# Moving a quarter of the retention's value projection into the turn after the first FFN, with the retention's first loads and key splits placed anew

## The chip, the cores and the metric

The kernel runs on one core of a Trainium2 chip. The metric is the device time of one execution in microseconds (us), as a median of runs. The engines are called as in the profile: PE is TensorE (PEld its weight loads), DVE is VectorE, ACT is ScalarE, POOL is GpSimd, SP is SyncE, which issues most DMAs.

## What is computed

One layer of an encoder on 1024 tokens of width 1024, float32 in and out. Cut to what matters here:

```python
h = swiglu(rms_norm(x), ffn1);  x = x + 0.5 * rms_norm(h)
u = rms_norm(x)
rq, rk, rv, rg, nq, nk, nv, g_ret, g_na = split(u @ w_mix_in)
y = bidirectional_retention(rotary(rq), rotary(rk), rv)   # 4 heads, keys 128, values 256
y_ret = (silu(rg) * headnorm(y)) @ w_ret_out
y_na  = neighbourhood_attention(nq, nk, nv) @ w_na_out     # 8 heads of 64
x = x + rms_norm((sigmoid(g_ret) * y_ret + sigmoid(g_na) * y_na) @ w_mix_out)
h = swiglu(rms_norm(x), ffn2);  x = x + 0.5 * rms_norm(h)
```

The retention runs over 8 chunks of 128 tokens a head, backward for the state that comes from later tokens and then forward.

## The kernel before

All float32 products are made of two parts a value: `split` (lines 61 to 63) writes a rounded high part with a cast on ACT (L62) and the rest as the low part with a subtraction on DVE (L63). `mm3` (L89 to L91) is one product: three matmuls, high by high, high by low and low by high. A weight piece of 128x512 comes by `raw` (L73, a DMA of 512 KB on the SP queue into a ring of four `wraw` buffers), and `load_w` splits it into two pieces, each in one of eight `wh` and eight `wl` buffers.

The work stands in stages: FFN 1 in and out (Winograd products of 2x2 blocks), **the turn**, the mixing projections `mx.run`, neighbourhood attention (`na_cores`), retention (`ret_cores`), output projections, FFN 2.

**The turn** is the stretch in which `ffn_out` has made its last product and the next projection needs the normalised and transposed x. `Epilogue.steps` (L661 to L681) normalises the rows of token tiles 4 to 7, adds the residual `xs[t]`, stores x1 (L670, an SP DMA) and normalises again (L680); `flip` (L128) transposes on PE; `Winograd.put` (L265 to L296) turns each transposed tile into the Winograd operands a22, s1 to s4, with eleven DVE and six ACT instructions a tile. The residuals `xs[t]` of tiles 4 to 7 are loaded by `xload` (L702) into `wraw` buffers, those of tiles 0 to 3 into the weight tiles of `ffn_out` that are no longer needed. Beside the flips runs a filler (`Filler`, a generator whose every step is one `mm3`): `first()` (L1330) makes the values nv of the attention for tokens 0 to 511 (32 steps, `vproj`) and the first products of `mx` (`leads`, 24 steps). FLIP_FILL says how many steps stand ahead of each of the four flips (8) and between a flip and its last split (2); the rest, 16 of the 56 steps, is drained behind them.

**Attention and retention** are fed with another filler, `products()` (L1410): the retention's values rv (`vproj(wrv[j], ...)`, two column halves j, token groups of 3, 3 and 2 tiles, 128 steps), then the gates (16 steps a row block, one `load_w` each), then the output projection of the attention. In all it has 384 steps. `na_cores` runs 32 units, takes 12 steps ahead and 2 + 2 a unit (NA_FILL), 148 in all. `ret_cores` takes what RET_FILL says: 14 at its start; in each head 2 ahead of the backward updates, 2 behind each of the seven updates, 4 and 2 ahead of the forward chunks, 3 and 1 in each of the eight chunks; that is 14 + 4 x 54 + 4 = 234. `fill.drain()` makes the last two.

A retention head needs: `kraw` and `qraw` (loaded by `load`, L1063, one buffer each), the transposed and decayed keys (`kdec.half(g)`: four transposes on PE, L1095, and splits with a scale on ACT and DVE, L65 and L66), the splits of keys and queries (`split_qk`), value chunks by `vget` (L1081 and a split). `half(1)` covers chunks 4 to 7, `half(0)` chunks 0 to 3. In the kernel before, `half(1)` of the next head stands in the last forward chunk, and `half(0)` at the head's start. In a forward chunk PE makes the scores of the next chunk, the filler's steps, the state update, and the cross and inner products; `norm` (L1125 to L1140) works on ACT, DVE and POOL.

The order within each engine's queue is not the text's order alone: Tile's scheduler issues whatever instruction of an engine is ready first by its own estimates, the earlier in the text having priority. SP's queue is one queue: a DMA that waits for its buffer holds up those behind it. Pools are stacked in SBUF; a tile of a new pool waits for the old tiles at its addresses.

Of the kernel before, what the change touches and what calls it, by code (L numbers as in the profile page):

```python
# [28 lines left out]
NHP = 4  # L29

NA_FILL = (12, 2, 2)
RET_FILL = (14, 2, 2, 4, 2, 3, 0, 1, 2)
FLIP_FILL = (8, 8, 8, 8, 2)
LOADS = (6, 9, 12, 15, 18, 22, 28, 33, 38)
NA_UNITS = ((0, 0, 0), (3, 1, 0), (1, 0, 1), (1, 0, 2), (4, 1, 1), (4, 1, 2), (2, 0, 3), (5, 1, 3))
KEY_OFF = (0, 8, 24, 32)
# [3 lines left out]
class Core:  # L40
# [4 lines left out]


    def __init__(self, tc, const, wpool, psum, dram):
        self.tc, self.nc = tc, tc.nc
        self.const, self.wpool, self.psum, self.dram = const, wpool, psum, dram
        nc = self.nc  # L50
        self.ident = const.tile([P, P], F32, name="ident")
        make_identity(nc, self.ident)
        self.mhalf = const.tile([P, 8], F32, name="mhalf")
        nc.gpsimd.memset(self.mhalf, -0.5)
        self.small = None
# [14 lines left out]

    def raw(self, src, n=D):
        raw = self.wpool.tile([P, D], F32, tag="wraw", name="wraw", bufs=4)
        self.nc.sync.dma_start(raw[:, :n], src)  # L73
        return raw

    def piece(self, src, eng=None):

# [332 lines left out]
class Pairs:  # L410
# [273 lines left out]
def ffn_out(c, tiles, q, blocks, w_out, gl, ep, tail, side={}):  # L684
# [16 lines left out]

    def xload(t):  # L702

        if t < 4 or ep.pre is None:
            tile = (tiles[0][1] + tiles[0][0])[t // 2]
            xs[t] = tile[:, t % 2 * 2:t % 2 * 2 + 2].rearrange("p k f -> p (k f)")
            nc.sync.dma_start(xs[t], ep.resid(t))
        else:
            xs[t] = c.raw(ep.resid(t))


    order = []
# [340 lines left out]
def ret_cores(c, pool, spool, d, dec, fill, n):  # L1053
# [2 lines left out]
    nc = c.nc  # L1056
    NC = TT

    def load(h):
        raw = {}  # L1060
        for q in "kq":
            raw[q] = pool.tile([P, S], F32, tag=f"{q}raw", name=f"{q}raw", bufs=1)
            nc.sync.dma_start(raw[q], d[f"r{q}"][h])  # L1063
        return raw

    def split_qk(raw):
# [7 lines left out]
    def vchunks(h):  # L1074
        vraw = {}

        def get(cc):
            if cc not in vraw:
                c0 = cc // 2 * 2
                vr = pool.tile([P, 2, 256], F32, tag="vraw", name="vraw", bufs=3)  # L1080
                nc.sync.dma_start(vr, d["rv"][c0:c0 + 2, :, h * 256:(h + 1) * 256].rearrange("c p d -> p c d"))  # L1081
                vraw[c0], vraw[c0 + 1] = vr[:, 0], vr[:, 1]
            v = [pool.tile([P, 256], F32R, tag=f"v{q}", name=f"v{q}", bufs=3) for q in "hl"]
            c.split(*v, vraw.pop(cc))
            return v
        return get

    def kdec(h, k):

        kd = [[pool.tile([P, NC, P], F32R, tag=f"kd{q}{b}", name=f"kd{q}{b}", bufs=1) for q in "hl"] for b in range(2)]  # L1090

        def half(g):
            pt = c.bank("pt", 2)
            for j in range(4):
                nc.tensor.transpose(pt[:, j * P:(j + 1) * P], k[:, (4 * g + j) * P:(4 * g + j + 1) * P], c.ident)  # L1095
# [54 lines left out]
        c.store(d["ry"][2 * h:2 * h + 2, :, cs].rearrange("k p t -> p k t"), rg)  # L1150

    left = []
    raw = load(0)
    fill(n[0])
    kd, half = kdec(0, raw["k"])
    half(1)
    for h in range(RH):
        fill(n[1])
        half(0)
        kf, kb = kd  # L1160
        sb = pool.tile([P, NC, 256], F32, tag="sb", name="sb", bufs=1)
        vget = vchunks(h)
        for cc in range(NC - 1, 0, -1):
            update(h, 1, kb, cc, vget(cc), sb[:, cc] if cc < NC - 1 else None, sb[:, cc - 1])
            fill(n[2])
            if left and cc < NC - 1:
                store(*left.pop(0))
            if cc == NC - 2:
                ops = split_qk(raw)
        raw = load(h + 1) if h + 1 < RH else None  # L1170
        fill(n[3])
        vget = vchunks(h)
        a = scores(h, ops, 0)
        v, sbs, st, sf = vget(0), state(sb[:, 0], "b"), None, None
        fill(n[4])
        for cc in range(NC):
            b = scores(h, ops, cc + 1) if cc < NC - 1 else None
            if cc == NC - 1 and raw:
                kd, half = kdec(h + 1, raw["k"])
                half(1)  # L1180
            fill(n[5])
            q = [o[:, cc * P:(cc + 1) * P] for o in ops["q"]]
            nsf = None
            if cc < NC - 1:
                old, st = st, pool.tile([P, 256], F32, tag="st", name="st", bufs=2)
                update(h, 0, kf, cc, v, old, st)
                nsf = state(st, "f")
            cross, inner = c.bank(), c.bank()[:, :256]
            if cc < NC - 1:
                c.mm3(cross[:, 256:], q, sbs, True, True)  # L1190
            c.mm3(inner, a, v, True, True)
            if cc > 0:
                c.mm3(cross[:, :256], q, sf, True, True)
            left.append((h, cc, norm(h, cc, cross, inner)))
            if cc < NC - 1:
                v = vget(cc + 1)
            if cc < NC - 2:
                sbs = state(sb[:, cc + 1], "b")
# [11 lines left out]
def trunk_layer(ctx: ExitStack, tc, x, xt, g1a, w1i, w1o, g1b, gma, wmt, wnv, wrv, logits, dtab, rope, bias,  # L1210
# [77 lines left out]

        return a21 if (t, k) == (1, 0) else wx.op(("a11", "a12", None, "a22")[2 * t + k])

    def vproj(src, groups, done):

        for toks in groups:
            banks = {t: c.bank() for t in toks}
            for k in range(KT):
                if k % 2 == 0:
                    w = ahead.pop(k // 2) if k // 2 in ahead else c.load_w(src[k // 2])
# [7 lines left out]
    evpool = []  # L1305

    def ev():
        return evpool[0].tile([P, S], F32, tag="ev", name="ev", bufs=3)

    def done_nv(t, b):  # L1310
        e = evpool[0].tile([P, 512], F32, tag="ev", name="ev", bufs=6 if len(evpool) == 1 else 4)
        nc.scalar.copy(e, b)  # L1312
        c.store(d["nv"][2 * t:2 * t + 2].rearrange("r c d -> (r c) d"), e)

    def done_rv(j):
        def f(t, b):
            e = ev()
            nc.scalar.copy(e[:, :512], b)
            c.store(d["rv"][t][:, j * 512:(j + 1) * 512], e[:, :512])
        return f  # L1320


# [5 lines left out]
    mx = Pairs(c, wx, [(wmt[j[0]], wmt[j[1]]) for j in jobs], 3)  # L1328

    def first():  # L1330
        yield from vproj(wnv, ((0, 1, 2, 3),), done_nv)
        yield from mx.leads()

    fill = Filler(first())
# [9 lines left out]
    with tc.tile_pool(name="pa", bufs=1, reuse_waits="tile") as pa:  # L1344
# [4 lines left out]
        def half():  # L1349
            return pa.tile([P, 512], F32, tag="ev", name="ev", bufs=6)  # L1350
# [42 lines left out]
    evpool[:] = [mix]  # L1393

    def gate(i, dst, halves=(0, 1)):

# [12 lines left out]

    def products():  # L1410
        for j in range(2):
            yield from vproj(wrv[j], ((0, 1, 2), (3, 4, 5), (6, 7)), done_rv(j))
        yield "rv"
        for i in range(4, 8):
            yield from gate(32 + i, d["sn"][i])
        for i in range(4):
            yield from gate(24 + i, d["sr"][i])
        for i in range(4, 8):
            yield from gate(24 + i, d["sr"][i], (1,))
        x1_stack.close()  # L1420
# [205 lines left out]
```

## Time and profile before

| what | us |
|---|---|
| median of 3 runs (2257.23 to 2262.26) | 2260.53 |
| the profiled execution's own time | 2262.09 |
| its span, first to last instruction | 2260.2 |
| PE busy | 2200.6 (97%) |
| DVE busy | 1638.3 (72%) |
| ACT busy | 984.0 (44%) |
| the turn | about 673 to 729 |
| attention | about 1004 to 1192 |
| retention | about 1192 to 1435 |

The page gives busy time by engine, the span in 40 slices, the chain of work that ended last, and groups of instructions. Further views of the same trace are used: busy time by windows (per engine: busy us and, in brackets, the number of instructions; PEclk is the granted clock of TensorE as a share of full speed), waits (engine, line, who ended the wait: us in total, times, longest), and the timeline of one engine (start, duration, line, operation, tiles, and in square brackets the idle time ahead of it and who ended it). Matmuls are pipelined, so a duration of 0.39 us is that of one; what counts on PE is the distance of their starts.

### The profile page before, as it was taken

What the parts mean: (1) busy time and instruction counts of PE and PEld (TensorE: products, weight loads), DVE (VectorE), ACT (ScalarE), POOL (GpSimd) and SP (SyncE); (2) the same over time, 40 slices, a digit from 0 to 9 for tenths busy, and PEclk for the clock granted to TensorE, in tenths of its full rate; (3) what the DMA queues carried; (4) which work ended last, traced back from release to release, by engine and by line L of the source; (5) the groups of instructions that cost most, each with busy time, mean ns of one, the idle gap of its engine ahead of it and who ended that gap; (6) DMA issues with size and microseconds to landing.
All of it is one profiled execution on the core that took longest, in us unless ns stands there. A gap on an engine that the chain in (4) does not pass through costs nothing.

```text
span 2260.2 us, 30006 instructions
## 1 busy us (share of the span) xinstructions
PE 2200.6 (97%) x10200; PEld 1827.2 (81%) x10200; DVE 1638.3 (72%) x2911; ACT 984.0 (44%) x2039; POOL 581.0 (26%) x755
## 2 busy tenths in 40 slices
PE   7899999999998999999999999999999999999998
PEld 5688888888786887878888888888887888888886
DVE  7898878765458757769885678553899887876444
ACT  5444434332334322248885665422544343433232
POOL 1121212158521122311101222111112121215942
PEclk9999999999999999999999999999999999999999
DMA  6354434497545455557655466686445443449864
GB/s 251 131 183 153 177 131 174 176 388 295 201 173 181 168 173 144 146 170 246 218 184 173 151 219 228 250 307 228 145 144 213 146 171 137 154 161 363 297 223 180
DMA packets 155240, 449.34 MB, mean 199 GB/s; under 512 B 19600, under 2 KB 50448, under 8 KB 152976
## 3 DMA queue, kind: packets, MB, share of 16 engines
q1 hardware_dynamic: 112656, 311.09, 39.9%
q0 software_dynamic: 42432, 136.35, 16.6%
q8 instruction: 81, 1.33, 0.2%
q14 instruction: 71, 0.58, 0.1%
HBM read 302.66 MB, written 148.90 MB: 200 GB/s over the span
## 4 chain that ended last, share of the span: by engine, by line
PE 84%; DVE 6%; issue 3%; ACT 3%; DMA 2%; POOL 2%; SPq 0%; POOLq 0%; DVEq 0%; ACTq 0%
PE ps L91 26%; PE ps L90 26%; PE ps L89 26%; PE pt L90 1%; PE pt L91 1%; PE pt L89 1%; POOL rstd L99 1%; DVE wl L63 1%; PE ps L921 1%; PE pt L940 1%; DMA wraw<-in_dram 1%; PE pt L128 0%; POOL ry L69 0%; ACT wh L62 0%; DVE s L922 0%
## 5 line engine op out<-in xcount | busy, mean ns | idle before, releaser
L63 DVE TENSOR_TENSOR wl<-wraw,wh 128x512 fp32r<-128x512 f32 x472 | 316.9, 688 | 63.1 <-ACT wh L62 62.7
L62 ACT CAST wh<-wraw 128x512 fp32r<-128x512 f32 x476 | 274.6, 618 | 175.1 <-PE ps L90 64.3
L89 PE MATMUL ps<-wh,g 128*128 128x512 f32 x548 | 214.1, 391 | 0.4 <-DVE tmp L226 0.4
L90 PE MATMUL ps<-wl,g 128*128 128x512 f32 x548 | 213.5, 390 | 0.0
L91 PE MATMUL ps<-wh,g 128*128 128x512 f32 x548 | 213.3, 389 | 0.0
L562 ACT ACTIVATE c<-c 128x512 f32<-128x512 f32 x88 | 55.4, 632 | 198.0 <-DVE c L527 103.9
L63 DVE TENSOR_TENSOR wl<-w,wh 128x512 fp32r<-128x512 f32 x77 | 76.0, 1005 | 88.3 <-ACT wh L62 88.1
L63 DVE TENSOR_TENSOR wl<-x,wh 128x512 fp32r<-128x512 f32 x77 | 79.2, 1044 | 76.2 <-ACT wh L62 74.8
L89 PEld LDWEIGHTS ps<-wh,g 128*128 128x128 f32 x548 | 102.9, 188 | 21.8 <-DVE tmp L226 0.7
L90 PEld LDWEIGHTS ps<-wl,g 128*128 128x128 f32 x548 | 102.9, 188 | 21.4 <-DVE wl L63 0.5
L91 PEld LDWEIGHTS ps<-wh,g 128*128 128x128 f32 x548 | 102.9, 188 | 21.2
L89 PE MATMUL ps<-a11h,wh 128*128 128x512 f32 x276 | 111.5, 404 | 8.4 <-ACT wh L62 8.4
L62 ACT CAST wh<-t 128x512 fp32r<-128x512 f32 x58 | 36.0, 621 | 190.0 <-DVE t L521 189.9
L91 PE MATMUL ps<-a11h,wl 128*128 128x512 f32 x276 | 109.8, 398 | 6.3 <-DVE wl L63 6.1
L90 PE MATMUL ps<-a11l,wh 128*128 128x512 f32 x276 | 109.7, 398 | 0.1
L91 PE MATMUL ps<-a22h,wl 128*128 128x512 f32 x280 | 109.2, 390 | 0.6 <-DVE wl L63 0.6
L89 PE MATMUL ps<-a22h,wh 128*128 128x512 f32 x280 | 109.7, 392 | 0.0
L89 PE MATMUL ps<-a12h,wh 128*128 128x512 f32 x276 | 108.9, 395 | 0.5 <-ACT ev L1312 0.3
L90 PE MATMUL ps<-a22l,wh 128*128 128x512 f32 x280 | 109.1, 390 | 0.0
L91 PE MATMUL ps<-a12h,wl 128*128 128x512 f32 x276 | 107.7, 390 | 0.0
L90 PE MATMUL ps<-a12l,wh 128*128 128x512 f32 x276 | 107.5, 390 | 0.0
L89 PE MATMUL ps<-s2h,wh 128*128 128x512 f32 x232 | 92.1, 397 | 7.0 <-ACT wh L62 7.0
(430 smaller groups left out, 6290.0 us busy)
## 6 DMA issues: line engine op xcount, KB each, us to landing
wraw<-in_dram SPq DMA_DIRECT2D x204, 512.0 KB, 4.4
g<-g0s SPq DMA_DIRECT2D x44, 512.0 KB, 4.1
g<-g1s SPq DMA_DIRECT2D x44, 512.0 KB, 4.9
g<-g0a SPq DMA_DIRECT2D x33, 512.0 KB, 3.3
g<-g1a SPq DMA_DIRECT2D x33, 512.0 KB, 4.3
g0s<-gth POOLq DMA_DIRECT2D x44, 256.0 KB, 4.7
g0s<-cmb POOLq DMA_DIRECT2D x44, 256.0 KB, 3.7
g1s<-gth POOLq DMA_DIRECT2D x44, 256.0 KB, 4.5
```

What stands on the lines that cost most here:

```text
L62: self.done = [nc.scalar.copy(h, src).ins, (eng or nc.vector).tensor_tensor(l, src, hf, ALU.subtract).ins]
L63: (eng or nc.vector).tensor_tensor(l, src, hf, ALU.subtract).ins]
L89: mm(ps, a[0], b[0], start=start, stop=False)
L90: mm(ps, a[0], b[1], start=False, stop=False)
L91: mm(ps, a[1], b[0], start=False, stop=stop)
L99: self.nc.gpsimd.tensor_tensor(r[:, :n], ms, self.mhalf[:, :n], ALU.pow)
L562: nc.scalar.activation(gate[j], gate[j], AF.Silu)
L921: nc.tensor.matmul(bv, q[:, rg * P:(rg + 1) * P], k, start=n == 0, stop=n == 1)
L940: nc.tensor.transpose(pt[:, j * P:(j + 1) * P], s[:, i % 2, (i // 2) * P:(i // 2 + 1) * P], c.ident)
```

## The change

It does five things. (1) `first()` also makes the values rv of column half 0 for tokens 0 to 511 (32 steps), and `products()` leaves them out: its first half now goes over tiles (4, 5) and (6, 7). The fill counts follow: FLIP_FILL is 12 ahead of each flip, and RET_FILL takes 4 at the start, 6 in place of 4 ahead of the forward chunks and 2 in place of 3 in a chunk, 4 + 4 x 48 + 4 = 200. (2) `xload` puts the residuals of tiles 4 to 7 into weight tiles of `ffn_out` (`tiles[1][0]`), not into `wraw` buffers. (3) `ret_cores` loads the first head's keys, two value blocks and queries in this order, with empty allocations between that set their addresses, and the next `raw` is ordered behind these loads on the SP queue (`hold`, `after`). (4) `half(0)` moves from the head's start to behind the second backward update. (5) `half(1)` of the next head moves from ahead of the last chunk's filler to behind its `norm`. `done_rv` takes its buffer as `done_nv` does (`half_ev`).

```diff
-RET_FILL = (14, 2, 2, 4, 2, 3, 0, 1, 2)
-FLIP_FILL = (8, 8, 8, 8, 2)
+RET_FILL = (4, 2, 2, 6, 2, 2, 0, 1, 2)
+FLIP_FILL = (12, 12, 12, 12, 2)
...
     def raw(self, src, n=D):
         raw = self.wpool.tile([P, D], F32, tag="wraw", name="wraw", bufs=4)
-        self.nc.sync.dma_start(raw[:, :n], src)
+        self.after(self.nc.sync.dma_start(raw[:, :n], src).ins, self.hold)
+        self.hold = []
         return raw
...
-        if t < 4 or ep.pre is None:
-            tile = (tiles[0][1] + tiles[0][0])[t // 2]
-            xs[t] = tile[:, t % 2 * 2:t % 2 * 2 + 2].rearrange("p k f -> p (k f)")
-            nc.sync.dma_start(xs[t], ep.resid(t))
-        else:
-            xs[t] = c.raw(ep.resid(t))
+        tile = (tiles[0][1] + tiles[0][0] if t < 4 or ep.pre is None else (None, None, *tiles[1][0]))[t // 2]
+        xs[t] = tile[:, t % 2 * 2:t % 2 * 2 + 2].rearrange("p k f -> p (k f)")
+        nc.sync.dma_start(xs[t], ep.resid(t))
...
+    vget = vchunks(0)
+
+    def between():
+        if loads[1:]:
+            return
+        vget.ahead(6)
+        for q in "hl":
+            pool.tile([P, 256], F32R, tag=f"v{q}", name=f"v{q}", bufs=3)
...
+    raw = load(0, between)
+    vget.ahead(4)
+    c.hold = list(loads)
     fill(n[0])
     kd, half = kdec(0, raw["k"])
     half(1)
     for h in range(RH):
         fill(n[1])
-        half(0)
...
             update(h, 1, kb, cc, vget(cc), sb[:, cc] if cc < NC - 1 else None, sb[:, cc - 1])
             fill(n[2])
+            if cc == NC - 2:
+                half(0)
...
             b = scores(h, ops, cc + 1) if cc < NC - 1 else None
-            if cc == NC - 1 and raw:
-                kd, half = kdec(h + 1, raw["k"])
-                half(1)
             fill(n[5])
...
             left.append((h, cc, norm(h, cc, cross, inner)))
+            if cc == NC - 1 and raw:
+                kd, half = kdec(h + 1, raw["k"])
+                half(1)
...
     def first():
-        yield from vproj(wnv, ((0, 1, 2, 3),), done_nv)
+        yield from vproj(wnv, ((0, 1, 2, 3),), done_nv, True)
+        yield from vproj(wrv[0], ((0, 1, 2, 3),), done_rv(0))
         yield from mx.leads()
...
         for j in range(2):
-            yield from vproj(wrv[j], ((0, 1, 2), (3, 4, 5), (6, 7)), done_rv(j))
+            yield from vproj(wrv[j], (((4, 5), (6, 7)), ((0, 1, 2), (3, 4, 5), (6, 7)))[j], done_rv(j))
```

More of the change, by code (lines that the diff above doesn't have):

```diff
@@ L47, in __init__ @@
     def __init__(self, tc, const, wpool, psum, dram):
-        self.tc, self.nc = tc, tc.nc
+        self.tc, self.nc, self.hold = tc, tc.nc, []
         self.const, self.wpool, self.psum, self.dram = const, wpool, psum, dram
@@ L72, in raw, with after @@
         raw = self.wpool.tile([P, D], F32, tag="wraw", name="wraw", bufs=4)
-        self.nc.sync.dma_start(raw[:, :n], src)
-        return raw
+        self.after(self.nc.sync.dma_start(raw[:, :n], src).ins, self.hold)
+        self.hold = []
+        return raw
+    def after(self, e, names):
+        for n in names:
+            self.tc.add_manual_dep(e, n, mybir.DependencyInfo(
+                mybir.DependencyClass.NoSync, mybir.DependencyReason.DATA), reason="order")
     def piece(self, src, eng=None):
@@ L1057, in ret_cores, with fetch, load @@
     NC = TT
-    def load(h):
+    loads = []
+    def fetch(t, src):
+        loads.append(nc.sync.dma_start(t, src).ins.name)
+    def load(h, between=lambda: None):
         raw = {}
@@ L1062, in load @@
             raw[q] = pool.tile([P, S], F32, tag=f"{q}raw", name=f"{q}raw", bufs=1)
-            nc.sync.dma_start(raw[q], d[f"r{q}"][h])
+            fetch(raw[q], d[f"r{q}"][h])
+            between()
         return raw
@@ L1075, in vchunks, with ahead @@
         vraw = {}
+        def ahead(c0):
+            vr = pool.tile([P, 2, 256], F32, tag="vraw", name="vraw", bufs=3)
+            fetch(vr, d["rv"][c0:c0 + 2, :, h * 256:(h + 1) * 256].rearrange("c p d -> p c d"))
+            vraw[c0], vraw[c0 + 1] = vr[:, 0], vr[:, 1]
         def get(cc):
             if cc not in vraw:
[L1079 to L1082, printed above, removed]
+                ahead(cc // 2 * 2)
             v = [pool.tile([P, 256], F32R, tag=f"v{q}", name=f"v{q}", bufs=3) for q in "hl"]
@@ L1085, in get @@
             return v
+        get.ahead = ahead
         return get
@@ L1152, in ret_cores @@
     left = []
-    raw = load(0)
+    vget = vchunks(0)
[5 more added lines that the diff above has]
+            pool.tile([P, 256], F32R, tag=f"v{q}", name=f"v{q}", bufs=3)
+        for q in ("st", "y"):
+            pool.tile([P, 256], F32, tag=q, name=q, bufs=2)
+        pool.tile([P, P], F32, tag="a", name="a", bufs=2)
+        for q in "hl":
+            pool.tile([P, P], F32R, tag=f"a{q}", name=f"a{q}", bufs=2)
+    raw = load(0, between)
+    vget.ahead(4)
+    c.hold = list(loads)
     fill(n[0])
@@ L1158, in ret_cores @@
         fill(n[1])
-        half(0)
         kf, kb = kd
         sb = pool.tile([P, NC, 256], F32, tag="sb", name="sb", bufs=1)
-        vget = vchunks(h)
+        vget = vget if h == 0 else vchunks(h)
         for cc in range(NC - 1, 0, -1):
@@ L1289, in xh, with vproj @@
         return a21 if (t, k) == (1, 0) else wx.op(("a11", "a12", None, "a22")[2 * t + k])
-    def vproj(src, groups, done):
+    def vproj(src, groups, done, begun=False):
         for toks in groups:
@@ L1296, in vproj @@
                 if k % 2 == 0:
-                    w = ahead.pop(k // 2) if k // 2 in ahead else c.load_w(src[k // 2])
+                    w = ahead.pop(k // 2) if begun and k // 2 in ahead else c.load_w(src[k // 2])
                 for t in toks:
@@ L1303, in vproj, with half_ev @@
                 done(t, banks[t])
-    evpool = []
+    evpool, mixing = [], "mixing"
     def ev():
         return evpool[0].tile([P, S], F32, tag="ev", name="ev", bufs=3)
+    def half_ev():
+        if evpool[-1] is mixing:
+            return ev()[:, :512]
+        return evpool[0].tile([P, 512], F32, tag="ev", name="ev", bufs=6 if len(evpool) == 1 else 4)
     def done_nv(t, b):
-        e = evpool[0].tile([P, 512], F32, tag="ev", name="ev", bufs=6 if len(evpool) == 1 else 4)
+        e = half_ev()
         nc.scalar.copy(e, b)
@@ L1316, in f @@
         def f(t, b):
-            e = ev()
-            nc.scalar.copy(e[:, :512], b)
-            c.store(d["rv"][t][:, j * 512:(j + 1) * 512], e[:, :512])
+            e = half_ev()
+            nc.scalar.copy(e, b)
+            c.store(d["rv"][t][:, j * 512:(j + 1) * 512], e)
         return f
@@ L1392, in trunk_layer @@
     mix.tile([P, 40], F32, name="pad")
-    evpool[:] = [mix]
+    evpool[:] = [mix, mixing]
     def gate(i, dst, halves=(0, 1)):
```

## The prediction

> **What bounds the kernel now.** First the page's busy times, then the windows, for where PE falls behind.
>
> ```profile
> PE 2200.6 (97%) x10200; PEld 1827.2 (81%) x10200; DVE 1638.3 (72%) x2911; ACT 984.0 (44%) x2039; POOL 581.0 (26%) x755
> 500.00:550.00 50.00, 50.00 (x222) 41.44 (x221) 27.01 (x23) 12.64 (x22) 42.08 (x29) 1.00 0.79 298
> 673.00:684.00 11.00, 11.00 (x55) 9.16 (x53) 9.48 (x18) 4.05 (x13) 3.34 (x6) 1.00 0.54 191
> 684.00:695.00 11.00, 6.25 (x23) 4.48 (x22) 8.64 (x16) 7.88 (x18) 2.06 (x3) 0.70 0.59 196
> 695.00:707.00 12.00, 11.97 (x57) 9.34 (x56) 11.07 (x20) 7.25 (x14) 1.26 (x2) 0.99 0.46 138
> 707.00:718.20 11.20, 7.25 (x32) 5.05 (x30) 10.93 (x20) 6.09 (x11) 2.37 (x4) 1.00 0.63 226
> 718.20:729.00 10.80, 10.76 (x40) 8.74 (x41) 10.21 (x17) 3.44 (x7) 0.56 (x1) 0.84 0.40 127
> ```
>
> Columns: PE, PEld, DVE, ACT, POOL busy with counts, the granted clock, DMA share, GB/s. PE bounds the kernel, so only its order and its gaps count. At full rate it starts 222 matmuls in 50.00 us, 0.225 us each; a filler step of three costs 0.676 us. The turn, 673 to 729, holds 56 steps (37.9 us) and 32 transposes, and takes 56 us. DVE is full from 684 on (40.9 of 45 us), PE idles 4.75 + 3.95 us in two windows, and the clock falls to 0.70 and 0.84.
>
> ```profile
> 653.32 0.87 PE pt L128 x8
> PE ps L89 <- ACT wh L62: 4.3, 1, 4.3
> PE ps L91 <- DVE wl L63: 3.7, 2, 3.4
> 669.29 5.14 SPq L670 DMA_DIRECT2D x<-wraw  x4
> 676.94 0.33 SPq L73 DMA_DIRECT2D wraw<-in_dram  x1
> 678.15 3.99 SPq L670 DMA_DIRECT2D x<-wraw  x4
> 683.05 19.91 SPq L73 DMA_DIRECT2D wraw<-in_dram  x5
> 682.91 0.62 ACT L62 CAST wh<-wraw 128x512 fp32r<-128x512 f32 x1 [3.31 <-DMA wraw<-in_dram]
> 717.50 1.28 DVE L63 TENSOR_TENSOR wl<-wraw,wh 128x512 fp32r<-128x512 f32 x2
> ```
>
> Eight transposes take 0.87 us on the chain of waits, so 32 take 3.5. The turn's PE work is 37.9 + 3.5 = 41.4 us; **14.6 us are lost**. The waits name two causes. The first, 4.3 us: the third weight block's load is issued at 676.94 and the fourth's at 683.05, among the stores of x1 from `wraw`: the four buffers of the ring hold residuals. The second, 3.4 us: a low half, ready only with the pair at 717.50, queued on DVE behind the Winograd operands.
>
> Attention and retention, by windows:
>
> ```profile
> 1003.90:1018.20 14.30, 11.49 (x51) 9.20 (x49) 9.43 (x31) 8.29 (x15) 0.54 (x1) 1.00 0.90 261
> 1018.20:1030.00 11.80, 10.59 (x42) 8.33 (x43) 10.63 (x42) 8.10 (x24) 1.07 (x2) 0.86 0.58 205
> 1030.00:1045.00 15.00, 14.11 (x84) 11.71 (x84) 14.41 (x41) 13.69 (x36) 3.47 (x4) 1.00 0.80 271
> 1225.40:1254.50 29.10, 29.10 (x179) 25.95 (x178) 21.55 (x62) 19.66 (x58) 8.05 (x12) 1.00 0.30 95
> 1338.00:1370.00 32.00, 30.81 (x182) 26.65 (x181) 25.51 (x70) 21.65 (x62) 9.62 (x13) 1.00 0.60 204
> PE pt L1148 <- DVE kdl L66: 1.8, 2, 1.1
> PE ps L89 <- DVE y L1133: 1.1, 2, 0.9
> PE pt L1095 <- DVE kdl L66: 0.6, 1, 0.6
> ```
>
> Attention's start is bound by the splits (DVE 14.41 and ACT 13.69 of 15). Retention is bound by PE in its first head, and waits 3.5 us in all in 1300 to 1400 (the last three rows): at the heads' seams for the decayed keys, in the third head for `norm`.
>
> **The change, part by part.** *Moved steps.* 32 steps leave attention and retention and stand in the turn: 32 x 0.676 = 21.6 us less there, 21.6 more here. The fill counts agree: attention takes 148 as before, retention 200 in place of 234, the drain 4 in place of 2. Both kernels load the values' weights in six groups of four blocks. So the sum on PE's work is zero, and the change is worth what it does to lost time.
>
> *The turn.* Its work becomes 63.0 us (88 steps, 32 transposes). Before, DVE had per flip 11 operand instructions and the splits of 10 steps, some 2.5, to do in 10 x 0.676 + 0.87 = 7.6 us; at 20 instructions in 11.07 us (row 695 to 707) these 13.5 take 7.5, no slack, and the backlog ends in the second wait. After, 14 steps stand on a flip: 10.3 us of PE, 14.5 instructions or 8.0 us of DVE. The backlog goes. The first wait goes too if the residuals no longer hold the ring: the blocks' DMAs can then be issued ahead of the stores, and the pieces are needed only at step 16, 673 + 16 x 0.676 + 0.87 = 684.7. What is late next: the two banks that the new values take over from nv, which ACT must copy out first, and the residuals' new places, which the operands s3 overwrite. The last of the eight stores is issued by 682.1 (678.15 + 3.99), and the first flip now stands at 673 + 12 x 0.676 = 681.1; a store of x1 took 5.07 us on the chain:
>
> ```profile
> 678.15 5.07 DMA x<-wraw
> PE ps L89 <- ACT ev L1312: 0.3, 1, 0.3
> ```
>
> So s3's first split may wait on ACT or DVE to about 687, some 2 us, with weight splits queued behind it; PE has pieces for 8 steps (5.4 us) in hand. A bank cost 0.3 us where it was seen. I leave 3 us of the 14.6 lost: **-11.6**. Bounds: -14.6, all lost time gone; -7, the first wait and its slow clock staying.
>
> *Attention's start.* Groups of two tiles need a weight block every 4 steps, not 6: in its first 32 steps 8 blocks, not 5.3; 1.7 of the additional ones fall behind 1018. Each is two splits on ACT and two on DVE (0.64 us each by the pair above): 2.2 us on an engine that is full there. Some of it stands in DVE's rest: **+1.5**, bounds 0 and +4 (2.2 and a slow clock).
>
> *Retention's start.* Its 14 steps covered late loads: SP waited with one weight DMA and `kraw` went out at 1192.27.
>
> ```profile
> 1173.03 19.08 SPq L73 DMA_DIRECT2D wraw<-in_dram  x2
> 1192.27 0.33 SPq L1063 DMA_DIRECT2D kraw<-rk  x1
> DMA to landing us min/median/max: 3.5/5.0/7.5
> 1203.92 0.69 ACT L65 ACTIVATE kdh<-pt,deck 128x512 fp32r<-128x512 f32 x1
> L66 DVE SCALAR_TENSOR_TENSOR kdl<-pt,deck,kdh 128x512 fp32r<-128x512 f32 x16 | 11.9, 748 | 6.0 <-ACT kdh L65 5.7
> ```
>
> After, 4 steps stand there. The loads stand ahead of that weight DMA, and their addresses are those of attention's first key, query and key operand tiles, which its last pair of heads no longer needs or leaves early; I take them as landed. From transposes to the first update stand two steps, 1.35 us, against the cast's 0.69, the low half's 0.75 and the hand-overs: **+0.4**, bounds 0 and +1.5.
>
> *Seams.* `half(0)` moves to where its keys are needed three updates later. `half(1)` has 3 steps (2.0 us) from its transposes to the next head's first update, and its cast stands near `norm` in ACT's queue. I take 1.2 us a seam, three seams, against 2.4 us of `kdl` waits now and the refill behind them: **+0.7**, bounds -2.4 and +7 (cast queued behind the whole `norm`).
>
> *Inside the chunks* a step goes, 0.68 us. A chunk has 29 PE instructions, 12 of the filler's and 17 small ones; by the row from 1225 (179 in 29.10 us) it takes 4.71. The ACT timeline of the first head:
>
> ```profile
> 1240.79 0.47 ACT L1131 ACTIVATE y<-ps,decq 128x256 f32<-128x256 f32 x1
> 1242.49 0.42 ACT L1136 ACTIVATE yn<-y 128x256 f32<-128x256 f32 x1 [1.24 <-DVE y L1134]
> 1243.97 0.51 ACT L1139 ACTIVATE yn<-y,rstd 128x256 f32<-128x256 f32 x1 [0.29 <-POOL rstd L99]
> 1244.39 0.39 ACT L62 CAST sbh<-sb 128x256 fp32r<-128x256 f32 x1
> 1244.68 0.40 ACT L62 CAST sfh<-st 128x256 fp32r<-128x256 f32 x1
> 1244.99 0.40 ACT L62 CAST vh<-vraw 128x256 fp32r<-128x256 f32 x1
> 1245.30 0.46 ACT L1131 ACTIVATE y<-ps,decq 128x256 f32<-128x256 f32 x1
> ```
>
> From one `y` to the next ACT goes through a closed loop, y to DVE, square, POOL's rstd, `yn`, three casts, `y`: 4.51 us. PE's chunk after is 4.03. If the order stays, the loop is the bound; if sb and sf, ready earlier, go ahead of `yn`, two starts of 0.30 us leave it, 3.9. I take the second in most chunks: **+2.0**, bounds -1.1 (today's waits gone) and 32 x 0.48 = +15.4.
>
> Sum: -11.6 + 1.5 + 0.4 + 0.7 + 2.0 = **-7.0 us**.
>
> **The rivals.**
> *A, the loop of ACT bounds the chunks* (slower). In its favour: in 1338 to 1370 PE already waits on it (30.81 of 32). Against: PE can run ahead within a head. It decides from 9.0 / 32 = 0.28 us a chunk on, where it has eaten the rest of the sum; in full it is 15.4 in place of 2.0, -7.0 + 13.4 = +6.4: 2267. The Trainium skill, *TensorE: Matmul & The Clock Gate*, section on the 32x32 sub-arrays, calls ACT's and DVE's queues strict FIFOs; by that rule no `y` passes a queued `yn`, as in the rows above, where each starts behind the one queued before.
> *B, gain given back.* The first wait stays (-7 in place of -11.6) and attention costs its +4: -7 + 4 + 0.4 + 0.7 + 2.0 = 0: 2260.5. For it: SP is one queue and waits 19.08 us in one place. Against: with the ring free the load waits on no store.
> *C, retention's loads don't come ahead*, held by an old tile. Then `kraw`, issued at 1192 and 5.0 us on its way (the median row above), leaves PE, with 2.7 us of steps, idle for some 4 with the hand-over: 2257.5.
> *D, retention takes the cut unharmed*: -11.6 + 1.5 - 1.1 - 2.4 = -13.6: 2247.
>
> **How the numbers follow.** The sum is made on the profiled execution: its span is 2260.2, its time 2262.09, 1.56 above the median of the runs. 2260.53 - 7.0 = **2253.5**. Chances: forecast 0.48 (2249.5 to 2257), A 0.14, B 0.17, C 0.08, D 0.13. From 2246 to 2264 all but A's greater part and the tails is held, 2 in 10 left out. A change of 0.2% (4.5 us) is about what a measurement can tell from none. Faster: D, and the forecast but for its upper end, 0.57; same: B, C, that end and the near part of A, 0.28; slower: 0.15.
>
> **What would show it.** Turn: 88 steps within about 66 us, no wait of PE over 1 us, clock near 1.00, the blocks' DMAs ahead of the x1 stores. Attention: `wl` waits of PE in 1018 to 1045. Retention: `kraw` issued before attention's end; distance of `y` to `y` under 4.2 us with PE full. Wrong is the forecast where the distance of `y` stays 4.5 and PE waits on L1133 in each chunk (A), or the first wait of the turn stays (B).

## The result and the profile after

The changed kernel takes 2269.25 us (median of 7 runs, 2265.58 to 2272.17), the kernel before 2260.53 (7 runs): ratio 1.0037, 95% interval 1.0027 to 1.0047. It is **slower by 8.4 us**; the forecast was 7.0 us faster. Its profiled execution has a span of 2270.4 us, 10.2 above that of before.

The turn first, in the page's busy row and the windows of the kernel after (PE, PEld, DVE, ACT, POOL, clock, DMA share, GB/s), then PE's only wait from 660 to 760 and SP's rows:

```profile
PE 2206.5 (97%) x10200; PEld 1830.7 (81%) x10200; DVE 1637.2 (72%) x2911; ACT 995.0 (44%) x2047; POOL 581.3 (26%) x755
```

```profile
684.00:695.00 11.00, 10.66 (x52) 8.74 (x51) 10.56 (x20) 5.41 (x10) 2.35 (x4) 1.00 0.35 121
...
707.00:718.20 11.20, 11.20 (x55) 9.36 (x54) 11.20 (x20) 6.12 (x12) 0.45 (x1) 1.00 0.50 171
718.20:729.00 10.80, 10.80 (x50) 8.93 (x49) 10.68 (x18) 7.23 (x14) 2.51 (x6) 1.00 0.72 254
729.00:737.60 8.60, 8.60 (x40) 7.12 (x39) 0.93 (x2) 0.62 (x1) 0.48 (x1) 1.00 0.48 154
```

```profile
PE pt L134 <- DVE cmb L297: 0.3, 1, 0.3
```

```profile
669.64 10.10 SPq L676 DMA_DIRECT2D x<-x  x6
680.90 0.33 SPq L73 DMA_DIRECT2D wraw<-in_dram  x1
```

The two holes of before (6.25 of 11.00 and 7.25 of 11.20 busy) are closed and the clock is 1.00. The turn ends at 737.6, 8.5 us later than before with 21.6 us more work in it. The weight load that went out at 676.94 now goes at 680.90: it isn't earlier, but the longer fill no longer needs it so soon.

The gain is gone by the end of retention. PE's waits in 1200 to 1450, where before had 3.5 us:

```profile
PE ps L95 <- DVE y L1145: 2.8, 5, 0.9
PE ps L95 <- ACT vh L62: 2.0, 1, 2.0
PE ps L97 <- DVE kdl L66: 2.0, 2, 1.7
PE ps L95 <- ACT ah L62: 1.7, 1, 1.7
PE pt L1160 <- ACT yn L1151: 1.3, 2, 0.7
PE ps L96 <- DVE xy L63: 1.2, 1, 1.2
```

Waits alone don't add up to the loss, since a slow clock follows some of them. So I sum **lost time**: the distance from each matmul's start to the next one's, less the distance at full rate (0.227 us at 512 columns, 0.178 at 384, 0.119 at 256, 0.111 at 128). "Chunks" runs in each head from the first scores to the last cross product, "first updates" from the first key transpose to head 0's scores, "tail" from the first output product on. In us, of the profiled executions:

| stage | before | after | e9 | e10 | e11 | e12 | e13 | forecast | measured |
|---|---|---|---|---|---|---|---|---|---|
| up to 660 | 29.0 | 29.2 | 27.1 | 26.3 | 27.5 | 26.7 | 26.4 | 0 | +0.2 |
| turn | 14.3 | 0.7 | 0.6 | 11.9 | 0.6 | 0.6 | 0.6 | -11.6 | -13.6 |
| mx and attention | 14.0 | 16.6 | 16.4 | 16.4 | 13.7 | 16.1 | 17.4 | +1.5 | +2.6 |
| head 0, first updates | 0.3 | 5.6 | 6.0 | 0.3 | 5.3 | 4.7 | 0.3 | +0.4 | +5.3 |
| heads 1 to 3, seams and updates | 3.4 | 7.1 | 4.5 | 0.5 | 6.1 | 3.2 | 0.5 | +0.7 | +3.7 |
| chunks | 3.6 | 11.7 | 9.4 | 1.3 | 3.6 | 2.7 | 1.3 | +2.0 | +8.1 |
| end of retention and tail | 6.1 | 10.0 | 10.7 | 4.6 | 7.9 | 7.3 | 4.5 | none | +3.9 |

The last two columns set the prediction's terms beside after less before; they sum to +10.2, the difference of the spans. Each column is one execution; that of after was the slowest of its seven, that of `e11` the fastest of its twelve. What chance does shows in rows with the same instructions: "up to 660" lies between 26.3 and 29.2, and the same mx and attention lose 14.0 in before and 16.4 in `e10`. So 2 or 3 us in the first and third row say nothing; the other rows differ by more between the kernels.

### The profile page after: what moved, and what is told of

It reads as the page before. It is cut to its first block, busy times and chain, and to the rows that moved or that the text cites. A ratio compares the mean times of both kernels' runs of the same rounds, so it can differ in the third digit from the quotient of the medians.

```text
span 2270.4 us, 30030 instructions
## 1 busy us (share of the span) xinstructions
PE 2206.5 (97%) x10200; PEld 1830.7 (81%) x10200; DVE 1637.2 (72%) x2911; ACT 995.0 (44%) x2047; POOL 581.3 (26%) x755
## 3 DMA queue, kind: packets, MB, share of 16 engines
q0 software_dynamic: 42432, 136.35, 16.6%
## 5 line engine op out<-in xcount | busy, mean ns | idle before, releaser
L96 PEld LDWEIGHTS ps<-wl,g 128*128 128x128 f32 x548 | 102.9, 188 | 21.6 <-DVE wl L63 0.5
```

The costliest lines, as they stand in the source:

```text
L96: mm(ps, a[0], b[1], start=False, stop=False)
```

## The experiments

The theory after the result: the turn pays as forecast, and the retention gives it back, because less of TensorE's work covers its chains. Its rivals: the turn pays less than its trace shows; or the early loads and moved key splits do the harm, by SP's queue.

In all ratios the kernel before, run on the same chip, is 1. An edit is shown against the kernel named.

**The turn.** `e1_ring` is the kernel before with the residuals in weight tiles alone; `e2_twice` is the turn of the kernel after on the retention and attention of before, so a quarter of the values is made twice, 21.6 us of excess work; `e5_twice_noring` is `e2_twice` with the residuals back in the ring.

```diff
 # e1_ring, against before
-        if t < 4 or ep.pre is None:
...
+        tile = (tiles[0][1] + tiles[0][0] if t < 4 or ep.pre is None else (None, None, *tiles[1][0]))[t // 2]
 # e2_twice, against after: loads and key splits as before, and
+RET_FILL = (14, 2, 2, 4, 2, 3, 0, 1, 2)
+            yield from vproj(wrv[j], ((0, 1, 2), (3, 4, 5), (6, 7)), done_rv(j))
 # e5_twice_noring, against e2_twice: xload as in the kernel before
```

> The kernel before with one edit of the change: the residuals of tiles 4 to 7 go into the weight tiles, not into the wraw ring. Theory 1 (the ring held back the third and fourth weight block): the turn's first wait of 4.3 us and the slow clock behind it go, the second wait of 3.4 us on DVE stays: 5 to 7 us faster, 2254 to 2256. Rival (DVE's backlog is all that counts, the wait only moves): within 2 us of 2260.5.

> The kernel after's turn alone, and the retention and its fill as before: the moved quarter of the values is made twice, at the turn and again by the filler in attention. So 32 steps of PE, 21.6 us, are in excess. Theory 1 (the turn takes in 13 us of them in its lost time): +8.5, 2269. Rival (the turn gains no more than its first wait, 6 us): +15.5, 2276. If it gains nothing: 2282.

> The kernel with the quarter made twice (2269.3), and the residuals of tiles 4 to 7 back in the wraw ring. Theory 1 (both edits are needed at the turn: the steps cover DVE, the free ring brings the weight blocks in time): the first wait of 4.3 us and its slow clock come back, 2274 to 2276. Rival (the longer fill alone does it, the third block then being needed 5 us later or its wait hidden): within 2 us of 2269.3.

Measured: `e1_ring` 2261.34, ratio 0.9993 (0.9985 to 1.0002); `e2_twice` 2269.30, 1.0033 (1.0020 to 1.0045); `e5_twice_noring` 2270.92, 1.0044 (1.0031 to 1.0056). The ring alone brings nothing. PE's waits of `e1_ring` in 660 to 740:

```profile
PE ps L91 <- DVE wl L63: 4.4, 1, 4.4
PE pt L128 <- ACT cmb L280: 3.4, 1, 3.4
```

The first wait, which ends at 691 as before, has only changed its name: it is now for ACT's operand `cmb`. The second is still for a low half. `e2_twice` costs 7.5 us by its ratio (8.2 by the medians) with 21.6 of additional work, so the turn takes in 13.4 to 14.1 us. With the residuals back in the ring (`e5_twice_noring`) some 2 us of that go: 2.5 by the ratios, whose intervals overlap, and PE waits 1.8 us for a low half. The **longer fill** does most of it, the ring little.

**The smaller fill alone**, on the kernel before (the 34 steps left over are drained at the end), and **the loads and key splits alone**: both (`e4_keys`), the loads (`e7_loads`), the splits (`e8_halves`).

```diff
 # e3_cut, against before
-RET_FILL = (14, 2, 2, 4, 2, 3, 0, 1, 2)
+RET_FILL = (4, 2, 2, 6, 2, 2, 0, 1, 2)
 # e4_keys and e7_loads, against before
-    raw = load(0)
+    raw = load(0, between)
+    vget.ahead(4)
+    c.hold = list(loads)
 # e4_keys and e8_halves, against before
-        half(0)
...
+            if cc == NC - 2:
+                half(0)
...
+                half(1)
```

> The kernel before with only the shorter fill counts of the retention (200 steps in place of 234; the 34 left are drained behind it, so PE's work is the same). Theory 1 (the shorter fill lays bare waits at the retention's start, in its chunks and at its seams): 12 to 19 us slower, 2272 to 2279, with some 3 us of the tail covered by the drain. Rival (the loss in the retention comes from the new order of loads and key splits): within 4 us of 2260.5.

> The kernel before with only the retention's first loads placed and issued ahead and the key splits moved, the fill counts, the values and the turn as before. Theory 1: within 3 us of 2260.5. Rival (the new order of loads and key splits is what costs): 8 to 18 us slower.

> The kernel before with the retention's first loads placed and issued ahead only; key splits where they were. Theory 1 (SP is one queue: a value load that waits for its buffer now stands ahead of the filler's weight blocks, and PE waits for a block at the retention's start): 2 to 5 us slower, 2263 to 2266. Rival (the key splits are what costs): within 2 us of 2260.5.

> The kernel before with the key splits moved only; the first loads as before. Theory 1 (the transposes behind norm leave too few steps before the first update, PE waits for kdh at two or three seams): 2 to 5 us slower, 2263 to 2266. Rival (spread splits take DVE's waits from the seams): 1 to 3 us faster.

Measured: `e3_cut` 2278.92, 1.0068 (1.0054 to 1.0083), some 15 us slower (its profiled execution took 5714.16 us, so no trace of it is used); `e4_keys` 2267.74, 1.0027 (1.0016 to 1.0037); `e7_loads` 2266.61, 1.0024 (1.0014 to 1.0033); `e8_halves` 2262.13, 1.0005 (0.9996 to 1.0014). So the parts made to soften the cut cost 6 us by themselves, nearly all of it the early loads: in `e7_loads` head 0's first updates lose 5.1 us in place of 0.3. PE's one wait in 1191 to 1226 there, and the windows around it:

```profile
PE ps L95 <- ACT wh L62: 3.2, 1, 3.2
```

```profile
1203.00:1206.40 3.40, 0.26 (x3) 0.02 (x1) 2.77 (x5) 3.40 (x8) 0.53 (x1) 1.00 0.86 216
1206.40:1208.00 1.60, 1.59 (x9) 1.50 (x10) 1.60 (x3) 1.41 (x4) 0.00 (x0) 0.78 0.98 379
1208.00:1210.20 2.20, 2.20 (x7) 1.71 (x7) 2.06 (x6) 1.98 (x6) 0.00 (x0) 0.50 0.64 259
```

PE stands for 3.2 us, and soon after it runs at half clock (0.50 in the last row).

**The turn without the cut.** `e6_job` keeps the turn of after and the whole retention of before. The 32 steps are made up elsewhere: two gate blocks are made as 32 filler steps in place of one Winograd job.

```diff
 # against e2_twice, with the values' split of after
-    jobs += [(32 + 2 * i, 33 + 2 * i, d["sn"][2 * i], d["sn"][2 * i + 1], AF.Sigmoid) for i in range(2)]
+    jobs += [(32 + 2 * i, 33 + 2 * i, d["sn"][2 * i], d["sn"][2 * i + 1], AF.Sigmoid) for i in range(1)]
-        for i in range(4, 8):
+        for i in range(2, 8):
             yield from gate(32 + i, d["sn"][i])
```

> The turn of the kernel after, the retention and its fill counts as before; what the filler loses to the turn it gets back from the mixing stage: one pair of gate blocks (sn 2 and 3) is made by the filler in 32 steps, not as a Winograd job of 84 matmuls. Theory 1 (the turn gains 13.4 us wherever the steps come from, and the retention keeps its cover): 96 in place of 84 matmuls cost 2.7 us, so 2260.5 - 13.4 + 2.7 = 2250, 2248 to 2253. Rival (every place from which steps are taken lays bare waits of its own, or the two more weight blocks crowd attention): 2256 or more.

Measured: 2252.56, 0.9963 (0.9950 to 0.9975), 8 us faster than before. The turn's gain is real when the retention keeps its fill.

**The loop of the chunks.** Theory: the norm's closed loop (rival A) bounds the chunks. ScalarE in the changed kernel, head 1:

```profile
1301.07 0.42 ACT L1148 ACTIVATE yn<-y 128x256 f32<-128x256 f32 x1 [0.23 <-DVE y L1146]
1301.39 0.18 ACT L1148 ACTIVATION_READ_ACCUMULATOR yn<-y 128x1 f32 x1
1301.49 0.28 ACT L62 CAST ah<-a 128x128 fp32r<-128x128 f32 x1
1302.57 0.51 ACT L1151 ACTIVATE yn<-y,rstd 128x256 f32<-128x256 f32 x1 [0.81 <-POOL rstd L105]
1302.99 0.39 ACT L62 CAST sbh<-sb 128x256 fp32r<-128x256 f32 x1
1303.29 0.40 ACT L62 CAST sfh<-st 128x256 fp32r<-128x256 f32 x1
1303.59 0.40 ACT L62 CAST vh<-vraw 128x256 fp32r<-128x256 f32 x1
1303.90 0.47 ACT L1143 ACTIVATE y<-ps,decq 128x256 f32<-128x256 f32 x1
1305.60 0.42 ACT L1148 ACTIVATE yn<-y 128x256 f32<-128x256 f32 x1 [1.23 <-DVE y L1146]
```

From square to square 4.53 us, against PE's chunk of 4.05. ACT idles 0.81 us for rstd with three casts and the next `y` queued behind. The edit puts a chunk's last scaling (`yn`) behind the next chunk's `y`; the rest is as it was. It is made on before (`e10_order_before`), on after (`e11_order`), and on `e9_oldfront`, which is after with loads and key splits at their old places (`e12_order_oldfront`).

```diff
-        nc.scalar.activation(yn, y, AF.Copy, scale=r[:, 0:1])
+        late.append(lambda: nc.scalar.activation(yn, y, AF.Copy, scale=r[:, 0:1]))
+        if cc == NC - 1:
+            late.pop()()
...
-            nc.scalar.activation(y, cross[:, :256], AF.Copy, scale=dec.qd[:, 0, h:h + 1])
+            e = nc.scalar.activation(y, cross[:, :256], AF.Copy, scale=dec.qd[:, 0, h:h + 1])
+            c.after(late.pop()().ins, [e.ins.name])
```

> The kernel after, with the retention's first loads and the key splits at the places of the kernel before: what is left of the change is the turn with its 32 steps of values and the retention's smaller fill. Theory 1, the parts add: the turn gives back 13.4 us (its lost matmul time, 14.1 less 0.7), the smaller fill by itself costs 15 to 18 (e3_cut), so the time is 2260.5 + 1.6 to 4.6, say 2263.5 (2260 to 2267), some 6 us faster than the kernel after. Rival: the early loads and late splits belong to the smaller fill and hide part of its loss, so without them the retention loses more: 2270 or above.

> The kernel before with one edit: the last step of the norm of a chunk (yn scaled by rstd on ScalarE) is put behind the next chunk's scaling of the cross product in ScalarE's queue, so that its wait for GpSimd's rstd holds nothing up. Control for e11_order. Theory 1, the loop Square, rstd, yn, three casts, y, two sums, Square of 4.53 us on ScalarE, VectorE and GpSimd bounds a chunk only when TensorE's own chunk is shorter; here it has three steps of fill and takes 4.73: no gain, ratio 0.9990 to 1.0005. Rival: the wait for rstd costs in any case, whatever the fill: 4 us or more faster.

> The kernel after with the same one edit. TensorE's chunk with two steps of fill is 4.05 us, the loop in ScalarE's queue 4.53; with yn behind y the loop is about 0.7 to the first cast, 0.9 of casts, 1.7 from y to Square, 3.3 in all, below TensorE's chunk. Theory 1, the loop causes the loss within the chunks (8 to 10 us of lost matmul time): 2269.3 less 8, 2261 (2258 to 2264.5). Rival: the chunks lose by late loads, banks and seams, and the loop only stands beside it: 2267 to 2271.

> e9_oldfront with the edit of e11_order. If both theories hold, the two gains add: 2263.5 less 8, 2255.5 (2252 to 2259), faster than both kernels. If the loop is not the cause, the time is that of e9_oldfront within 2 us. If the early loads were needed, 2262 or above.

Measured: `e9_oldfront` 2265.36, 1.0019 (1.0010 to 1.0029); `e10_order_before` 2253.23, 0.9968 (0.9956 to 0.9980); `e11_order` 2259.30, 0.9997 (0.9989 to 1.0006); `e12_order_oldfront` 2254.77, 0.9969 (0.9957 to 0.9981). ScalarE in `e11_order`:

```profile
1295.33 0.42 ACT L1149 ACTIVATE yn<-y 128x256 f32<-128x256 f32 x1
...
1296.70 0.41 ACT L62 CAST sbh<-sb 128x256 fp32r<-128x256 f32 x1 [0.67 <-PE ps L97]
1297.01 0.40 ACT L62 CAST sfh<-st 128x256 fp32r<-128x256 f32 x1
1297.32 0.40 ACT L62 CAST vh<-vraw 128x256 fp32r<-128x256 f32 x1
1297.63 0.47 ACT L1143 ACTIVATE y<-ps,decq 128x256 f32<-128x256 f32 x1
1297.99 0.50 ACT L1152 ACTIVATE yn<-y,rstd 128x256 f32<-128x256 f32 x1
1299.33 0.42 ACT L1149 ACTIVATE yn<-y 128x256 f32<-128x256 f32 x1 [0.83 <-DVE y L1147]
```

Square to square is 4.00 us, and what ACT waits for is now PE. The chunks' loss falls from 11.7 to 3.6 us, in the pair `e9`, `e12` from 9.4 to 2.7. So the loop is shown as the cause of most of what the chunks lose. But my control failed: the same edit gains 7 us on the kernel before too, where I had expected nothing from a loop of 4.51 under a chunk of 4.71. There it takes away the third head's 2.6 us and the waits on `kdl` behind it (chunks 3.6 to 1.3, seams 3.4 to 0.5), 5.2 of the 7 us. Where other casts join the loop it is longer than PE's chunk with full fill as well; ACT and PE in the third head of the kernel before:

```profile
1340.50 0.42 ACT L1136 ACTIVATE yn<-y 128x256 f32<-128x256 f32 x1 [0.85 <-DVE y L1134]
...
1344.48 1.12 ACT L62 CAST wh<-wraw 128x512 fp32r<-128x512 f32 x2
...
1347.84 0.42 ACT L1136 ACTIVATE yn<-y 128x256 f32<-128x256 f32 x1 [0.44 <-DVE y L1134]
```

```profile
1347.20 0.39 PE L89 MATMUL ps<-vh,ah 128*128 128x256 f32 x1 [0.90 <-DVE y L1133]
```

From square to square 7.34 us, with five weight casts between them, and PE waits for `y`. Of the 9 to 10 us that the edit gains on after, 7 were to be had before the change.

`e9_oldfront` against after: 4 us of the 8.4 are the early loads and late splits, also beside the cut. Not as much as alone (6), for head 0's first updates lose 6.0 us by the cut itself.

**Both gains together.** `e13_job_order` is `e6_job` with the reordered `yn`.

> e6_job (the turn of the kernel after, the retention as before with its full fill, the 32 steps made up by two gate blocks that leave the Winograd jobs for the filler) with the reordered yn. Theory: the turn's 8 us and the norm's 7 us lie in different stages and add: 2252.6 less 7.3 = 2245.3 (2242 to 2248.5). Rival, the reorder's gain on the kernel before is not in the retention alone (its profiled run also lost 2.4 us less in the turn, which the edit does not touch), so that part is missing here: 2249 or above.

Measured: 2249.26 (2244.96 to 2251.69), 0.9948 (0.9936 to 0.9960), **faster than both kernels**, 12 us under before. The lost times add as expected (turn 0.6, retention free of waits of PE from 1180 to 1450), the medians not quite: 0.37% and 0.32% apart, 0.52% together. The missing 0.17% is less than the errors of the three together, so it need not be real.

**Head 0's first updates.** `e14_start` gives `e12_order_oldfront` its first 14 steps back. `e15_values5` takes the wait of the value loads on SP away in `e7_loads`, by two more buffers. `e16_apart` (on `e15_values5`) and `e17_apart_order3` (on `e11_order`) put the second four key transposes behind filler steps or behind two updates; `e18_apart_order` adds the five buffers to the latter.

```diff
 # e14_start
-RET_FILL = (4, 2, 2, 6, 2, 2, 0, 1, 2)
+RET_FILL = (14, 2, 2, 6, 2, 2, 0, 1, 2)
 # e15_values5, e18_apart_order
-            vr = pool.tile([P, 2, 256], F32, tag="vraw", name="vraw", bufs=3)
+            vr = pool.tile([P, 2, 256], F32, tag="vraw", name="vraw", bufs=5)
 # e16_apart; e17 and e18 with the last matmul of the second update in place of c.last
+                if (h, g) == (0, 0):
+                    c.after(e.ins, [c.last])
```

> e12_oldfront's order kernel with the retention's first fill at 14 steps, as in the kernel before, in place of 4; the filler then runs out ten steps (6.8 us) earlier, in the last head. Theory 1, the 4.7 us that the first head's update phase loses there (0.3 in the kernel before) come from the steps missing at its start: that phase's loss falls under 1 us, the last head and the end pay 1 to 3 us for it: 2254.8 less 2.5 = 2252.3 (2250 to 2254). Rival, the loss stands where the values' first splits wait for their loads, whatever the fill: update phase still above 4 us and the time 2254 or more.

> e7_loads (the kernel before with the first loads early only, 2266.6) with five buffers of the values' loads in place of three, so that the value loads queued ahead of the second weight block on SP have a buffer and need not wait for a split (19.1 us in e7_loads). Theory 1, the head of SP's queue: the weight block goes out 19 us earlier, the wait of 3.2 us on wh and the slow clock behind it are gone, 4.8 us of loss in the first update phase: 2266.6 less 4.8 = 2261.8 (2260 to 2264). Rival, the weight block is held by its own ring or by the DMA traffic, and nothing changes: 2265 to 2268.

> e15_values5 (the kernel before with the first loads early and five value buffers, 2265.8) with the second four key transposes of the first head put two filler steps behind the first four in TensorE's queue, as they stand in the kernel before, in place of all eight in one row. Theory 1: with eight in a row ScalarE casts all four blocks of decayed keys and a query half ahead of the next weight cast, and TensorE's next step waits 3.15 us for it, with some 1.6 us of slow clock behind; apart, the weight cast stands behind two of them, and most of the 5.2 us of that phase goes: 2265.8 less 4 = 2261.8 (2259.5 to 2263.5). Rival, the wait is one for ScalarE's total work there, and only moves by some steps: 2264.5 or more.

> e11_order (the kernel after with the reordered yn, 2259.3) with the second four key transposes put behind the first two updates in TensorE's queue. Theory 1, the row of eight transposes causes the 5.3 us lost in the first head's update phase: 2259.3 less 3.5 = 2255.8 (2253.5 to 2257.5). Rival, here the start lacks cover (two filler steps between keys and first update) and the weight block queued on SP behind the waiting value loads: 2258 or more.

> e17_apart_order3 with five buffers of the values' loads in place of three, so that the weight blocks on SP no longer stand behind a value load that waits 22 us for its buffer. If SP's queue costs beside the casts' order: 2 to 3 us below e17_apart_order3. By e15_values5, where the earlier block changed nothing (2265.8 against 2266.6): within 1.5 us of it.

Measured: `e14_start` 2254.89, 0.9979 (0.9970 to 0.9987): the phase's loss is gone (4.7 to 0.3), so the missing first steps were its cover. But the filler now runs out early: the third head's chunks and the end of retention lose 6 us more, and nothing is gained. `e15_values5` 2265.80, 1.0020 (1.0010 to 1.0030): no difference to `e7_loads` that the intervals would show. SP's row of `e7_loads`, then of `e15_values5`:

```profile
1200.53 0.46 SPq L73 DMA_DIRECT2D wraw<-in_dram  x1
```

```profile
1185.28 0.46 SPq L73 DMA_DIRECT2D wraw<-in_dram  x1
```

The second weight block goes out 15 us earlier, and PE still waits 3.15 us for its cast. SP's queue, which I had blamed, is not the cause of this wait. What stands ahead of that cast in ScalarE's queue, in `e15_values5`, and then in the kernel before:

```profile
1205.02 0.60 ACT L1442 ACTIVATE ev<-ps 128x512 f32<-128x512 f32 x1 [3.21 <-PE ps L97]
1205.52 1.26 ACT L65 ACTIVATE kdh<-pt,deck 128x512 fp32r<-128x512 f32 x2
1206.66 0.63 ACT L62 CAST qh<-qraw 128x512 fp32r<-128x512 f32 x1
1207.16 1.29 ACT L65 ACTIVATE kdh<-pt,deck 128x512 fp32r<-128x512 f32 x2
1208.32 1.16 ACT L62 CAST wh<-wraw 128x512 fp32r<-128x512 f32 x2
```

```profile
1202.40 0.62 ACT L62 CAST wh<-wraw 128x512 fp32r<-128x512 f32 x1 [1.06 <-PE ps L90]
1202.92 0.59 ACT L1406 ACTIVATE ev<-ps 128x512 f32<-128x512 f32 x1
```

With early loads the cast `wh` stands behind `ev`, which waits 3.21 us for PE's last filler matmul, and behind four key casts and a query cast; in the kernel before it stands ahead of `ev`. Taking the row of transposes apart did not help: `e16_apart` 2263.62, 1.0010 (1.0001 to 1.0019), still loses 5.0 us in that phase; `e17_apart_order3` 2259.35, 0.9994 (0.9985 to 1.0003), and `e18_apart_order` 2261.54, 0.9999 (0.9990 to 1.0008), both no better than `e11_order`, with 5.9 and 4.4 us lost (`e18_apart_order` loses 7.4 in the third head's chunks, `e11_order` 2.7). So neither SP's queue nor the transposes' row is the main cause. That the order of ScalarE's queue is, the traces of `e7_loads` and `e15_values5` suggest; a kernel with the weight's cast put ahead of `ev` was not tried, and it **stays open**. Nor would it hold for after: there, and in `e9_oldfront` without early loads, PE waits in this phase for a values' cast, `vh` (2.0 and 2.2 us).

## Why the prediction was wrong, by its steps

*Moved steps and the turn* (-11.6): right in size (-13.6; `e2_twice` 13.4 to 14.1), and with bounds that held. The cause was half right: I credited the first wait's end to the free ring, which would let the blocks' loads go ahead of the stores of x1. The block's load went at 680.90, behind six of the eight stores, and `e1_ring` shows that without the longer fill the wait stays.

*Attention's start* (+1.5, bounds 0 and +4): +2.6, in the bounds, but not more than chance does in that row, so it is neither shown nor refuted.

*Inside the chunks* (+2.0): **this step failed**. I had measured the loop at 4.51 us against a chunk of 4.03, and then assumed that sb and sf would go ahead of `yn` "in most chunks". They don't: the rows of after have the same order, `yn`, three casts, `y`, and the loop takes 4.53. That was rival A, which had a chance of 0.14. It cost 8.1 us, not its full 15.4, as PE's lead lasts for most of a head: in head 0 the chunks start at 1231 and lose nothing before 1258.9. `e11_order` shows it by taking it away. The waits of before that the prediction counted as a possible gain (1.1 in the chunks, 2.4 at the seams) hung on the same loop: `e10_order_before` is without them.

*Retention's start* (+0.4, bounds 0 and +1.5): failed too, +5.3. I asked whether the keys were there in time, and they were: `kraw` was issued at 1183.51, before attention's end at 1203.2. I set one key cast and one low half, 0.69 and 0.75 us, against two steps. But ScalarE has a whole row of casts ahead of the one that PE waits for (`vh`, 2.0 us above):

```profile
1212.79 0.69 ACT L65 ACTIVATE kdh<-pt,deck 128x512 fp32r<-128x512 f32 x1 [2.90 <-PE pt L1107]
...
1217.07 0.72 ACT L62 CAST vh<-vraw 128x256 fp32r<-128x256 f32 x2
```

Between these rows stand, without a pause, three more key casts, two of values, two of queries and a copy. 14 steps of fill covered them (`e14_start`).

*Seams* (+0.7, bounds -2.4 and +7): +3.7, in the bounds, mis-sized. `e8_halves` loses 2.2 us more than before at the seams, from the splits' new places; its time, 1.1 us longer by the ratio, can't be told from none.

*No term* stood for the end of retention and the first output products: +3.9 us. Two of the waits listed above stand there: for the last chunks' `yn` (1.3) and for the first split of the output projection (`xy`, 1.2). With the loop cut the first is gone, but `e11_order` still has 1.8 of the 3.9; where it comes from is open.

Between the sum of -7.0 and the +10.2 of the spans lie 17.2 us: the chunks have 6.1 of them, retention's start 4.9, the missing term 3.9, the seams 3.0, the other rows -0.7. Apart from that, the prediction's chances for the verdicts don't fit together: slower has 0.15, more than all of A (0.14), though a part of A is counted under same.

One at a time, by the ratios, turn -14.1, cut +15.4, loads +5.4 and splits +1.1 make +7.8, against +8.4 measured. Each part is known to 2 or 3 us only, so that they come so close is partly luck. Turn and cut together are `e9_oldfront`, +4.3 in place of +1.3, and loads and splits beside them cost 4.1 in place of 6.5; the errors could make these differences too. For the second the table has a reason: cut and loads lose the same time at head 0's start (6.0 in `e9_oldfront`, 5.1 in `e7_loads`, 5.6 together).

## What to carry to other kernels

Work that fills PE beside a chain of small operations is not only work: it is the cover of that chain, and moving it away uncovers the loop. Where a loop in the trace is longer than the chunk will be, count on it as the bound unless the order in the queue is changed by the edit itself (here 8.1 of the 15.4 us that it could cost came). And look first whether the loop can be shortened: one instruction put behind another in ScalarE's queue brought 7 us, as much as the whole forecast.

## What the runs showed of the hardware

A stop of PE costs more than itself. Windows of `e7_loads` behind the stop of 3.15 us, which ends at 1206.41, and of `e12_order_oldfront` around its three waits in the same phase (1.21, 0.50 and 0.44 us):

```profile
1206.20:1207.28 1.08, 0.87 (x5) 0.78 (x6) 1.08 (x3) 1.08 (x3) 0.00 (x0) 1.00 0.89 311
1207.28:1210.69 3.41, 3.41 (x12) 2.82 (x12) 3.27 (x8) 2.99 (x9) 0.00 (x0) 0.50 0.78 278
1210.69:1214.00 3.31, 3.31 (x18) 2.78 (x17) 1.51 (x3) 0.59 (x2) 0.00 (x0) 1.00 0.90 302
```

```profile
1210.82:1214.23 3.41, 1.34 (x5) 0.51 (x3) 3.41 (x7) 3.41 (x9) 0.00 (x0) 1.00 0.59 198
1214.23:1217.64 3.41, 3.34 (x12) 2.99 (x13) 2.86 (x8) 2.41 (x7) 0.53 (x1) 0.50 0.51 143
1217.64:1221.00 3.36, 3.36 (x20) 2.88 (x20) 2.71 (x6) 0.41 (x1) 0.00 (x0) 1.00 1.00 369
```

In both the clock is still 1.00 while PE waits (and in `e7_loads` for 0.87 us after), then 0.50 for 3.41 us, then 1.00 again. By these rows that is worth an estimated 1.7 us (half of 3.41); with the 3.15 it makes 4.9 of the 5.1 us lost. No single long stop is needed: in `e12_order_oldfront` the longest is 1.21 us, and PE is busy for 1.34 of the 3.41 us ahead. The Trainium skill, *TensorE: Matmul & The Clock Gate*, Part 1, lists two states of the clock, full and half, and says that a monitor sets the share by how busy PE has recently been. The 1.00 and 0.50 of these rows agree.

SP's queue may stand for 19 us behind a load that waits for its buffer (`e7_loads`) without a cost that shows: with that wait gone the time was 2265.80 us, with it 2266.61, and the intervals don't tell them apart.
